# A hybrid encoder block: smaller first weight pieces, another load order and fewer zero products at the begin

## The chip, the cores and the metric

The kernel runs on one core of a Trainium2 chip. The metric is the device time of one execution in microseconds (us). Three runs of the kernel before took 1491.58, 1492.98 and 1494.12 us; the median is 1492.98 us.

## What is computed

The reference is one layer of an encoder trunk on 256 tokens of 2048 features, all in float32:

```python
u = _rms_norm(x, norm_mix_pre[l])
mix = hybrid_mixer(u, w_in[l], ...)          # proj = u @ w_in, three attention-like branches, @ w_out
x = x + _rms_norm(mix, norm_mix_post[l])
hdn = jnp.square(jax.nn.relu(_rms_norm(x, norm_mlp_pre[l]) @ w_mlp_up[l]))
x = x + _rms_norm(hdn @ w_mlp_down[l], norm_mlp_post[l])
```

Inside the mixer, `u @ w_in` gives the queries, keys and values of a stick-breaking attention and of a forgetting attention, the inputs of an RWKV-7 time mixing, and three gates. This case is about the first three column groups of that product only: 128 columns of `w_in` each, which are three heads of the stick-breaking queries.

## The kernel before

**Number format.** Every matrix product is made from float32 parts that TensorE reads in a shorter format. A weight tile `raw` (128 partitions x 1024 columns, 512 KB) is turned by ScalarE into a rounded copy `whi` (L158, at the begin L331) and by VectorE into the rest `wlo` = raw - whi (L159, at the begin L332). The activations are treated alike: `xsplit(k)` (L317) makes from feature tile k of x (128 features x 256 tokens) a tile `pk` of 512 columns, the rounded half by ScalarE (L242) and the rest by VectorE (L243). A full product is then `whi` with 512 columns of `pk` (a "hi" product, L340 at the begin) plus `wlo` with the first 256 columns (a "lo" product, L338).

**Staging.** All weights lie in one stack `wst` of 512 KB tiles in the order of use. A group of 128 output columns, a "unit", needs two tiles: one for the feature tiles 0 to 7, one for 8 to 15. In the steady part the helper `wnext` keeps one split weight tile ahead of TensorE, and SyncE's DMA queue (SP) loads three raw tiles ahead. VectorE, ScalarE and TensorE work side by side, and TensorE's order is the program's order.

**The begin.** x arrives in feature tiles and nothing is loaded yet. The first three units therefore share the feature tiles as they come: weight tiles 0, 2 and 4 hold the first halves of units 0, 1 and 2, tiles 1, 3 and 5 the second halves. The loop at L342 goes through the first eight feature tiles in two rounds of four. In a round, all three units take their 512-column piece of tiles 0, 2 and 4: `wpart(n, q)` splits the piece, `prods(n, ks, low)` issues one product for each feature tile. So a round has 12 hi and 12 lo products. Then each unit takes feature tiles 8 to 15 with its second weight tile (L358 to L371), unit 0 first: it needs feature tiles 8 to 15 split by VectorE one after the other.

**What sets the order.** The engines work through their queues in program order, and each piece of work waits for what it reads. SP issues the loads one after the other (L271 to L301): the parameters, the first pieces of weight tiles 0, 2, 4 (256 KB each), feature tiles 4 to 7 (512 KB), the second pieces, feature tiles 8 to 11, weight tile 1, and so on. ScalarE's own DMA queue issues feature tiles 0 and 1 and then 2 and 3 (L272). Eight counters are shared in turn by the DMAs of both queues, and a DMA waits at its issue for the one eight places before it.

**Zero products.** While nothing has arrived, TensorE multiplies a zeroed float32 tile by itself (L280): seven products of 256 columns, each of which the profile shows as two instructions. Their result is not used.

Of the kernel before, what the change touches and what calls it, by code (L numbers as in the profile page):

```python
# [17 lines left out]
T = 256  # L18
# [5 lines left out]
HALF = 1024  # L24
# [26 lines left out]
def hybrid_block(ctx, tc, xt, x, gains, params, consts, lora, gup, wst, out):  # L51
    nc = tc.nc
    V, A, G, PE = nc.vector, nc.scalar, nc.gpsimd, nc.tensor
# [11 lines left out]
    def nm(s):  # L65
        uid[0] += 1
        return f"{s}_{uid[0]}"
# [4 lines left out]
    def mps():  # L72
        return pm.tile([128, 512], F32, tag="mps", name=nm("mps"), bufs=4)
# [194 lines left out]
    def loadx(a, b, queue=nc.sync):  # L268
        return queue.dma_start(out=X0[:, a:b, :], in_=xt[:, a:b, :])

    nc.sync.dma_start(out=par, in_=params)  # L271
    for a in (0, 2):  # L272
        first_x = loadx(a, a + 2, nc.scalar)
    with tc.issue_after(first_x.ins):
        warm = A.activation(dum, dum, AF.Tanh)
    A6 = rp.tile([128, 6, T], F32, tag="b6", name="a6", bufs=1)
    zt = rp.tile([128, T], F32, tag="tha", name="zt", bufs=1)
    V.memset(zt, 0.0)
    idle = mps()
    for i in range(7):  # L280
        PE.matmul(idle[:, 0:T], zt[:, 0:128], zt, start=True, stop=True)
    raws = {}

    def load(n, q=None):

        if n not in raws:
            raws[n] = (rp.tile([128, HALF], F32, tag="m", name=nm("raw"), bufs=4) if n % 2 else
                       wpool.tile([128, HALF], F32, tag="raw", name=nm("raw"), bufs=3))
        cs = slice(0, HALF) if q is None else slice(512 * q, 512 * q + 512)
        nc.sync.dma_start(out=raws[n][:, cs], in_=wst[n][:, cs])  # L290

    for n in (0, 2, 4):
        load(n, 0)
    loadx(4, 8)
    for n in (0, 2, 4):
        load(n, 1)
    loadx(8, 12)
    load(1)
    loadx(12, 16)
    for n in (3, 5):  # L300
# [16 lines left out]
    def xsplit(k):  # L317
        u = pk()
        split(X0[:, k, :], u, P("g1", k))
        upk.append(u)  # L320
# [1 line left out]
    qb = [gps() for _ in range(3)]  # L322
    w = {}

    def wpart(n, q):
        if n not in w:
            w[n] = (wpool.tile([128, HALF], F32R, tag="whi", name=nm("whi"), bufs=3),
                    wpool.tile([128, HALF], F32R, tag="wlo", name=nm("wlo"), bufs=3))
        hi, lo = w[n]
        cs = slice(512 * q, 512 * q + 512)  # L330
        A.activation(hi[:, cs], raws[n][:, cs], AF.Copy)  # L331
        V.tensor_tensor(lo[:, cs], raws[n][:, cs], hi[:, cs].bitcast(F32), ALU.subtract)  # L332

    def prods(n, ks, low):
        for k in ks:
            i = k % 8
            if low:
                PE.matmul(qb[n // 2][:, 0:T], w[n][1][:, i * 128:i * 128 + 128], upk[k][:, 0:T], start=False, stop=k == 15)  # L338
            else:
                PE.matmul(qb[n // 2], w[n][0][:, i * 128:i * 128 + 128], upk[k], start=k == 0, stop=False)  # L340

    for q in range(2):  # L342
        ks = range(4 * q, 4 * q + 4)
        for k in ks[0:2]:
            xsplit(k)
        wpart(0, q)
        prods(0, ks[0:2], False)
        for k in ks[2:4]:
            xsplit(k)
        prods(0, ks[2:4], False)  # L350
        wpart(2, q)
        prods(2, ks, False)
        prods(0, ks, True)
        wpart(4, q)
        prods(4, ks, False)
        prods(2, ks, True)
        prods(4, ks, True)
    for k in range(8, 12):  # L358
        xsplit(k)
    for q in range(2):  # L360
        wpart(1, q)
    prods(1, range(8, 12), False)
    for k in range(12, 16):
        xsplit(k)
# [1 line left out]
    prods(1, range(8, 16), True)  # L366
    for n in (3, 5):
        for q in range(2):
            wpart(n, q)
        prods(n, range(8, 16), False)  # L370
        prods(n, range(8, 16), True)  # L371
    wpos[0] = 6
# [702 lines left out]
    c0 = g0 + 80  # L1075
# [558 lines left out]
    for g in range(4):  # L1634
# [8 lines left out]
        for tt, ps in enumerate(tok(hp, 3 if g == 3 else 1)):  # L1643
# [25 lines left out]
            with tc.issue_after(added.ins):  # L1669
                for c in (1024, 1536):  # L1670
                    cs = slice(c, c + 512)
# [131 lines left out]
```

## Time and the profile before

| what | value |
|---|---|
| median of three runs | 1492.98 us |
| the profiled execution | 1491.24 us, of which the span of its instructions is 1489.5 us |
| TensorE (PE) busy | 1476.4 us, 99% of the span |
| VectorE (DVE) busy | 1214.5 us, 82% |
| ScalarE (ACT) busy | 933.4 us, 63% |
| mean granted TensorE clock | 0.998 of full speed |

Times in the rows below are counted from the first instruction of the span. The profile names the engines PE (products), PEld (its weight loads), DVE, ACT, POOL and SP; a "q" behind an engine's name is its issuing part. The time between the span and the execution's own time, 1.74 us, lies before and after the kernel's instructions.

### The profile page before, as it was taken

What the parts mean: (1) busy time and instruction counts of PE and PEld (TensorE: products, weight loads), DVE (VectorE), ACT (ScalarE), POOL (GpSimd) and SP (SyncE); (2) the same over time, 40 slices, a digit from 0 to 9 for tenths busy, and PEclk for the clock granted to TensorE, in tenths of its full rate; (3) what the DMA queues carried; (4) which work ended last, traced back from release to release, by engine and by line L of the source; (5) the groups of instructions that cost most, each with busy time, mean ns of one, the idle gap of its engine ahead of it and who ended that gap; (6) DMA issues with size and microseconds to landing.
All of it is one profiled execution on the core that took longest, in us unless ns stands there. A gap on an engine that the chain in (4) does not pass through costs nothing.

```text
span 1489.5 us, 22848 instructions
## 1 busy us (share of the span) xinstructions
PE 1476.4 (99%) x8427; PEld 1248.4 (84%) x8427; DVE 1214.5 (82%) x1688; ACT 933.4 (63%) x1394; POOL 90.0 (6%) x160
## 2 busy tenths in 40 slices
PE   9999999999999999999999999999999999999997
PEld 8888888888778888788888888888888888888885
DVE  7676778999678898567647788999899999999986
ACT  7465666654576554474444777776767767777653
POOL 0011000100001100000000000000000000000000
PEclk9999999999999999999999999999999999999999
DMA  7545454545544546445855768888888887989874
GB/s 285 189 164 183 161 177 169 184 159 198 174 148 167 183 164 208 142 158 189 272 193 207 273 209 254 255 257 255 247 255 251 267 256 223 260 249 283 259 249 155
DMA packets 107759, 317.70 MB, mean 213 GB/s; under 512 B 10752, under 2 KB 14976, under 8 KB 107392
## 3 DMA queue, kind: packets, MB, share of 16 engines
q1 hardware_dynamic: 94688, 284.39, 55.4%
q0 software_dynamic: 8064, 29.36, 10.6%
q10 hardware_dynamic: 4896, 2.49, 0.6%
q8 instruction: 66, 1.08, 0.3%
q14 instruction: 45, 0.37, 0.1%
HBM read 282.65 MB, written 4.19 MB: 193 GB/s over the span
## 4 chain that ended last, share of the span: by engine, by line
PE 98%; DVE 1%; DMA 0%; issue 0%; ACT 0%; POOLq 0%; POOL 0%; DVEq 0%; ACTq 0%
PE gps L220 28%; PE gps L174 23%; PE gps L178 13%; PE gps L204 7%; PE mps L1511 3%; PE mps L1512 3%; PE mps L1513 3%; PE gps L1511 3%; PE gps L1513 3%; PE gps L1512 3%; PE gps L182 2%; PE gps L340 1%; PE mps L828 1%; PE gps L1270 0%; PE gps L338 0%; DMA x<-in_xt_dram 0%
## 5 line engine op out<-in xcount | busy, mean ns | idle before, releaser
L159 DVE TENSOR_TENSOR wlo<-raw,whi 128x1024 fp32r<-128x1024 f32 x495 | 600.9, 1221 | 154.2 <-ACT whi L158 139.4
L158 ACT ACTIVATE whi<-raw 128x1024 fp32r<-128x1024 f32 x495 | 521.5, 1057 | 253.9 <-PE gps L220 87.4
L174 PE MATMUL gps<-pk,whi 128*128 128x512 f32 x1321 | 332.4, 392 | 0.0
L220 PE MATMUL gps<-whi,pk 128*128 128x512 f32 x1136 | 286.4, 392 | 0.0
L174 PEld LDWEIGHTS gps<-pk,whi 128*128 128x128 f32 x1321 | 244.7, 188 | 47.6
L220 PEld LDWEIGHTS gps<-whi,pk 128*128 128x128 f32 x1136 | 211.4, 188 | 44.1 <-issue 0.4
L178 PEld LDWEIGHTS gps<-pk,wlo 128*128 128x128 f32 x1408 | 192.0, 190 | 13.6
L178 PE MATMUL gps<-pk,wlo 128*128 128x256 f32 x1408 | 196.9, 283 | 0.0
L220 PE MATMUL gps<-wlo,pk 128*128 128x512 f32 x568 | 155.3, 392 | 0.0
L220 PEld LDWEIGHTS gps<-wlo,pk 128*128 128x128 f32 x568 | 105.7, 188 | 22.0
L1374 DVE TENSOR_TENSOR sp<-raw,sp 128x1024 fp32r<-128x1024 f32 x67 | 81.7, 1220 | 3.4 <-ACT sp L1373 3.1
L1402 ACT ACTIVATE sp<-gps 128x512 f32<-128x512 f32 x52 | 31.1, 598 | 84.3 <-PE gps L182 84.3
L1373 ACT ACTIVATE sp<-raw 128x1024 fp32r<-128x1024 f32 x67 | 70.7, 1055 | 14.1 <-PE mps L1512 5.1
L204 PE MATMUL gps<-whi,pk 128*128 128x512 f32 x256 | 68.9, 390 | 0.0
L1511 PE MATMUL mps<-whi,fm 128*128 128x512 f32 x168 | 66.2, 394 | 0.0
L1512 PE MATMUL mps<-whi,fm 128*128 128x512 f32 x168 | 65.8, 392 | 0.0
L1513 PE MATMUL mps<-wlo,fm 128*128 128x512 f32 x168 | 65.6, 390 | 0.0
L1473 POOL DMA_DIRECT2D raw<-raw x40 | 35.0, 874 | 427.4 <-DVE raw L1470 108.4
L204 PEld LDWEIGHTS gps<-whi,pk 128*128 128x128 f32 x256 | 47.8, 188 | 9.9
L1511 PE MATMUL gps<-whi,fm 128*128 128x512 f32 x126 | 49.3, 391 | 0.0
L1513 PE MATMUL gps<-wlo,fm 128*128 128x512 f32 x126 | 49.1, 390 | 0.0
L1470 DVE TENSOR_TENSOR raw<-raw,raw 128x1024 f32<-128x1024 f32 x40 | 48.8, 1220 | 0.4
(400 smaller groups left out, 2013.4 us busy)
## 6 DMA issues: line engine op xcount, KB each, us to landing
raw<-in_wst_dram SPq DMA_DIRECT2D x499, 512.0 KB, 4.4
raw<-raw POOLq DMA_DIRECT2D x40, 512.0 KB, 6.4
sp<-in_wst_dram SPq DMA_DIRECT2D x16, 512.0 KB, 5.3
raw<-sp POOLq DMA_DIRECT2D x8, 512.0 KB, 6.2
sp<-raw POOLq DMA_DIRECT2D x8, 512.0 KB, 6.4
x<-in_x_dram SPq DMA_DIRECT2D x8, 256.0 KB, 5.5
xs<-x SPq DMA_DIRECT2D x2, 1024.0 KB, 4.8
x<-xs SPq DMA_DIRECT2D x4, 512.0 KB, 6.5
```

The source lines that it names most:

```text
L158: A.activation(hi, raw, AF.Copy)
L159: V.tensor_tensor(lo, raw, hi.bitcast(F32), ALU.subtract)
L174: PE.matmul(ps, hi[:, i * 128:i * 128 + 128], pks[i], start=first and i == 0, stop=False)
L178: PE.matmul(ps[:, 0:T], lo[:, i * 128:i * 128 + 128], pks[i][:, 0:T], start=False, stop=False)
L204: PE.matmul(ps[tt], pks[k][:, c:c + 128], w[:, (k - k0) * 512:(k - k0) * 512 + 512], start=k == 0 and part == 0 and w is hl[0], stop=w is ...
L220: PE.matmul(ps[tt], pks[k][:, c:c + 128], w[:, (k - k0) * 512:(k - k0) * 512 + 512], start=k == 0 and part == 0 and w is hl[0], stop=False)
L1373: A.activation(hi, raw, AF.Copy)
L1374: V.tensor_tensor(lo, raw, hi.bitcast(F32), ALU.subtract)
L1470: V.tensor_tensor(x, x, z, ALU.add)
L1511: PE.matmul(Q[f], p, w, start=d == 0 and i == 0, stop=False)
L1512: PE.matmul(Q[f], pl, w, start=False, stop=False)
L1513: PE.matmul(Q[f], p, wl, start=False, stop=d == nd - 1 and i == 1)
```

## The change

Feature tiles 2 and 3 are loaded by SP instead of ScalarE's queue. The first 512 columns of weight tiles 0, 2 and 4 are loaded and split in two pieces of 256 columns (128 KB) each, and the order of SP's loads is: first pieces, feature tiles 2 and 3, second pieces, feature tiles 4 to 7, third pieces (512 columns). The loop over rounds now has three rounds, of two, two and four feature tiles. The zero products are four of 256 columns and one of 128. The sum of products and of bytes is the same.

```diff
-    for a in (0, 2):
-        first_x = loadx(a, a + 2, nc.scalar)
+    first_x = loadx(0, 2, nc.scalar)
@@
-    for i in range(7):
-        PE.matmul(idle[:, 0:T], zt[:, 0:128], zt, start=True, stop=True)
+    for i in range(5):
+        PE.matmul(idle[:, 0:T // (1 + i // 4)], zt[:, 0:128], zt[:, 0:T // (1 + i // 4)], start=True, stop=True)
@@
-    def load(n, q=None):
+    def load(n, c0=0, c1=HALF):
...
-        cs = slice(0, HALF) if q is None else slice(512 * q, 512 * q + 512)
+        cs = slice(c0, c1)
         nc.sync.dma_start(out=raws[n][:, cs], in_=wst[n][:, cs])
 
     for n in (0, 2, 4):
-        load(n, 0)
+        load(n, 0, 256)
+    loadx(2, 4)
+    for n in (0, 2, 4):
+        load(n, 256, 512)
     loadx(4, 8)
     for n in (0, 2, 4):
-        load(n, 1)
+        load(n, 512)
     loadx(8, 12)
@@
-    def wpart(n, q):
+    def wpart(n, c0, c1):
...
-        cs = slice(512 * q, 512 * q + 512)
+        cs = slice(c0, c1)
@@
-    for q in range(2):
-        ks = range(4 * q, 4 * q + 4)
+    for k0, k1 in ((0, 2), (2, 4), (4, 8)):
+        ks = range(k0, k1)
         for k in ks[0:2]:
             xsplit(k)
-        wpart(0, q)
+        wpart(0, 128 * k0, 128 * k1)
         prods(0, ks[0:2], False)
-        for k in ks[2:4]:
+        for k in ks[2:]:
             xsplit(k)
-        prods(0, ks[2:4], False)
-        wpart(2, q)
+        prods(0, ks[2:], False)
+        wpart(2, 128 * k0, 128 * k1)
         prods(2, ks, False)
         prods(0, ks, True)
-        wpart(4, q)
+        wpart(4, 128 * k0, 128 * k1)
         prods(4, ks, False)
         prods(2, ks, True)
         prods(4, ks, True)
```

SP's queue before, from its first load to the last piece of the second round (raw_101, raw_103 and raw_105 are weight tiles 0, 2 and 4; x_85 holds all feature tiles, 512 columns being two of them):

```order
L271 DMA par<-in_params_dram 128x116
L290 DMA raw_101<-in_wst_dram 128x512
L290 DMA raw_103<-in_wst_dram 128x512
L290 DMA raw_105<-in_wst_dram 128x512
L269 DMA x_85<-in_xt_dram 128x1024
L290 DMA raw_101<-in_wst_dram 128x512
L290 DMA raw_103<-in_wst_dram 128x512
L290 DMA raw_105<-in_wst_dram 128x512
```

The same stretch of SP's queue after the change (raw_98, raw_100 and raw_102 are weight tiles 0, 2 and 4):

```order
L271 DMA par<-in_params_dram 128x116
L289 DMA raw_98<-in_wst_dram 128x256
L289 DMA raw_100<-in_wst_dram 128x256
L289 DMA raw_102<-in_wst_dram 128x256
L269 DMA x_85<-in_xt_dram 128x512
L289 DMA raw_98<-in_wst_dram 128x256
L289 DMA raw_100<-in_wst_dram 128x256
L289 DMA raw_102<-in_wst_dram 128x256
L269 DMA x_85<-in_xt_dram 128x1024
L289 DMA raw_98<-in_wst_dram 128x512
L289 DMA raw_100<-in_wst_dram 128x512
L289 DMA raw_102<-in_wst_dram 128x512
```

Feature tiles 4 to 7 (128x1024) have moved from the fifth place to the ninth.

ScalarE before, from feature tile 2 to the first piece of the second round (pk tiles are the split feature tiles):

```order
L242 ACTIVATE pk_144<-x_85,par 128x256
L242 ACTIVATE pk_147<-x_85,par 128x256
L331 ACTIVATE whi_152<-raw_103 128x512
L331 ACTIVATE whi_164<-raw_105 128x512
L242 ACTIVATE pk_180<-x_85,par 128x256
L242 ACTIVATE pk_183<-x_85,par 128x256
L331 ACTIVATE whi_138<-raw_101 128x512
```

ScalarE after the change, from feature tile 2 to the first piece of the third round:

```order
L242 ACTIVATE pk_163<-x_85,par 128x256
L242 ACTIVATE pk_166<-x_85,par 128x256
L333 ACTIVATE whi_139<-raw_98 128x256
L333 ACTIVATE whi_145<-raw_100 128x256
L333 ACTIVATE whi_153<-raw_102 128x256
L242 ACTIVATE pk_187<-x_85,par 128x256
L242 ACTIVATE pk_190<-x_85,par 128x256
L333 ACTIVATE whi_139<-raw_98 128x512
```

Three pieces of 256 columns stand where two of 512 stood, and from feature tile 4 (pk_180 before, pk_187 now) the order is the old one, on VectorE too. Behind the begin no engine's order differs.

## Rows read from the trace of the kernel before

**Rows 1.** The page, busy time of each engine and its instructions.

```profile
PE 1476.4 (99%) x8427; PEld 1248.4 (84%) x8427; DVE 1214.5 (82%) x1688; ACT 933.4 (63%) x1394; POOL 90.0 (6%) x160
```

**Rows 2.** Waits of PE, whole span: waiter, releaser, us in total, times, longest.

```profile
PE gps L340 <- DVE pk L243: 0.9, 1, 0.9
PE mps L1255 <- DVE x L1217: 0.5, 1, 0.5
```

**Rows 3.** The chain that ended last, 0 to 80 us: start us, us, what.

```profile
1.18 5.59 DMA x<-in_xt_dram
...
7.88 1.82 PE gps L340 x6
...
12.06 1.84 PE gps L340 x8
```

**Rows 4.** Timeline of ACT, 0.7 to 18.9 us: start us, us, what, idle time before.

```profile
3.58 0.91 ACT L242 ACTIVATE pk<-x,par 128x256 fp32r<-128x256 f32 x2 [0.42 <-DMA x<-in_xt_dram]
5.37 0.63 ACT L331 ACTIVATE whi<-raw 128x512 fp32r<-128x512 f32 x1 [0.88 <-DMA raw<-in_wst_dram]
6.80 0.91 ACT L242 ACTIVATE pk<-x,par 128x256 fp32r<-128x256 f32 x2 [0.80 <-DMA x<-in_xt_dram]
...
8.99 0.91 ACT L242 ACTIVATE pk<-x,par 128x256 fp32r<-128x256 f32 x2 [0.24 <-DMA x<-in_xt_dram]
9.81 0.61 ACT L331 ACTIVATE whi<-raw 128x512 fp32r<-128x512 f32 x1
...
12.19 1.71 ACT L242 ACTIVATE pk<-x,par 128x256 fp32r<-128x256 f32 x4
```

**Rows 5.** Timeline of DVE, 0.8 to 19 us.

```profile
4.12 0.89 DVE L243 SCALAR_TENSOR_TENSOR pk<-x,par,pk 128x256 fp32r<-128x256 f32 x2 [0.46 <-ACT pk L242]
...
8.26 1.29 DVE L332 TENSOR_TENSOR wlo<-raw,whi 128x512 fp32r<-128x512 f32 x2
9.54 0.88 DVE L243 SCALAR_TENSOR_TENSOR pk<-x,par,pk 128x256 fp32r<-128x256 f32 x2
...
11.06 0.88 DVE L243 SCALAR_TENSOR_TENSOR pk<-x,par,pk 128x256 fp32r<-128x256 f32 x2
...
15.85 1.67 DVE L243 SCALAR_TENSOR_TENSOR pk<-x,par,pk 128x256 fp32r<-128x256 f32 x4
```

**Rows 6.** Timeline of PE, 0 to 19 us.

```profile
1.18 5.38 PE L281 MATMUL mps<-zt 128*128 128x256 f32 x14 [1.18 <-DVE zt L278]
...
11.90 2.00 PE L340 MATMUL gps<-pk,whi 128*128 128x512 f32 x8
...
16.09 2.01 PE L340 MATMUL gps<-pk,whi 128*128 128x512 f32 x8
```

**Rows 7.** Windows: us, busy of PE, PEld, DVE, ACT, POOL, PEclk, DMA share, GB/s.

```profile
0.00:3.50 3.50, 2.32 (x6) 1.87 (x7) 0.54 (x4) 1.49 (x2) 2.18 (x15) 1.00 0.45 135
3.50:6.50 3.00, 3.00 (x11) 2.51 (x10) 1.52 (x4) 1.54 (x3) 0.00 (x0) 1.00 0.98 298
6.50:9.00 2.50, 1.65 (x7) 0.91 (x6) 1.84 (x5) 1.95 (x5) 0.00 (x0) 1.00 1.02 370
...
12.00:17.00 5.00, 5.00 (x29) 4.34 (x28) 5.00 (x11) 5.00 (x13) 0.00 (x0) 1.00 1.02 419
```

**Rows 8.** Timeline of SP, 0 to 9.4 us: the issues of its DMAs.

```profile
1.17 1.37 SPq L290 DMA_DIRECT2D raw<-in_wst_dram  x3
2.58 0.44 SPq L269 DMA_DIRECT2D x<-in_xt_dram  x1
3.06 1.72 SPq L290 DMA_DIRECT2D raw<-in_wst_dram  x3
```

**Rows 9.** The tile of x, 0 to 15 us: time of its DMAs from issue to landing.

```profile
DMA to landing us min/median/max: 2.8/6.4/7.5
```

**Rows 10.** The line of the zero products: duration in ns min/median/max, first and last start.

```profile
L281 PE MATMUL mps<-zt x14: 378/634/792, 1.2 to 6.2; 128*128 128x256 f32 x14
```

**Rows 11.** Timeline of PE, 3.0 to 5.1 us.

```profile
2.62 2.77 PE L281 MATMUL mps<-zt 128*128 128x256 f32 x6
```

More of the change, by code (lines that the diff above doesn't have):

```diff
@@ L360, in hybrid_block @@
     for q in range(2):
-        wpart(1, q)
+        wpart(1, 512 * q, 512 * q + 512)
     prods(1, range(8, 12), False)
@@ L368, in hybrid_block @@
         for q in range(2):
-            wpart(n, q)
+            wpart(n, 512 * q, 512 * q + 512)
         prods(n, range(8, 16), False)
```

## The prediction

> **What bounds the kernel now.** I read the busy times first. TensorE is busy for 1476.4 of 1489.5 us [rows 1], so only 13 us of the span could be won without removing products. The waits of TensorE come next: apart from its start they are 0.9 us at the first products, at 7.88 us, and 0.5 us at L1255, far behind this change [rows 2]. The chain of work that ended last agrees. It runs through the load of x, from 1.18 to 6.78 us, through the split of feature tiles 2 and 3, and from 7.88 us through TensorE [rows 3]. So whatever the change brings must come from the time before 7.88 us, and it must survive the stretch in which TensorE still waits for freshly made operands.
>
> What feeds TensorE there is read in the timelines. ScalarE waits for feature tile 0 until 3.58, for the first weight piece until 5.37, for feature tile 2 until 6.80 and for feature tile 4 until 8.99 us [rows 4]. Each of these waits ends with a landing. From 8.99 us on it goes on without a gap, and VectorE from 9.54 us: in the window from 12 to 17 us both are busy for 5.00 of 5.00 us [rows 4, 5, 7]. So there are two limits in turn, the loads up to feature tile 4, and ScalarE and VectorE behind it. TensorE does not show the second one, because it starts late enough.
>
> **Unchanged work.** A hi product takes 1.84 / 8 = 0.23 us [rows 3]. A round of four feature tiles takes 16.09 - 11.90 = 4.19 us [rows 6]. The three new rounds hold the same products, the first two together 4.19 us and the third another 4.19 us. No byte is added.
>
> **Zero products.** At first their records start (2.77 - 0.634) / 5 = 0.427 us apart [rows 10, 11]. The change leaves nine of the fourteen records, the ninth at the same pace as the others or shorter. They end at about 1.18 + 9 x 0.427 + 0.2 (pipeline, 0.634 - 0.427) = 5.2 us, where they now last until 6.56 us [rows 6]. Cutting them saves nothing by itself. Kept at seven, they would hold the first product until 6.2 us, and that would be hidden behind round 3, as shown below.
>
> **Rounds 1 and 2: cost nothing, gain nothing that lasts.** By the windows 3.5 x 135 = 472 kB have moved by 3.5 us, 298 GB/s follow until 6.5 us and 370 GB/s until 9 us [rows 7]. Feature tiles 4 to 7 are the last of 1850 KB = 1894 kB: parameters 58 KB, feature tiles 0 to 3 512 KB, pieces 768 KB, and their own 512 KB. By those rates 1894 kB have moved at 6.5 + (1894 - 1366) / 370 = 7.93 us, and ScalarE starts on them at 8.99 [rows 4]: landing comes 1.06 us after the mean byte. With the same rates and lag the changed order lands the first pieces at 4.5, 4.9 and 5.4 us, feature tiles 2 and 3 at 6.25 and the second pieces at 6.7, 7.1 and 7.6 us. Splitting two feature tiles takes ScalarE 0.91 us [rows 4]. A 256-column piece is not in these rows. It lies between half of the 0.61 us of 512 columns and all of it; I take 0.4, near the half. VectorE has the second feature tile split at 4.12 + 0.89 = 5.01 us [rows 5]. So the first product comes at about 5.2 us, round 1 ends at 7.3, round 2 starts at 7.55 and ends at about 9.65 us. At the upper price ScalarE would be through at 8.8 and VectorE at 9.4 us, both before feature tile 4 needs them at 8.99 and 9.54. So more instructions, at either price, cost nothing.
>
> **Round 3: where the gain is taken back.** It needs feature tiles 4 to 7, as the old second round did, and the order on ScalarE and VectorE from there is the old one. If they land when they did, the first weight piece is ready at 9.81 + 0.61 = 10.42 us [rows 4]. TensorE waits from 9.65 to 10.46. Feature tiles 6 and 7 are split on VectorE at 11.54 and 11.94 us (11.06 + 0.48, then 0.40 more) [rows 5]. So the fourth product starts at 11.98, and the rest of the round, 4.19 - 3 x 0.23 = 3.50 us, ends at 15.48 instead of 16.09. That is 0.61 us ahead. Then unit 0 takes feature tiles 8 to 15. VectorE ends the last of them at 15.85 + 1.67 = 17.52 us [rows 5], so its product starts at 17.56; before, it started at 16.09 + 7 x 0.23 = 17.70 [rows 6]. Only 0.14 us is left. The 2.5 us by which TensorE could start earlier are used up by a VectorE that was full already. **The gain is 0.14 us plus whatever feature tiles 4 to 7, and what follows them, land earlier.**
>
> **How much earlier do they land?** The bytes ahead of them are the same, so only the rate counts. The alternation of two queues ends earlier, since feature tiles 2 and 3 leave ScalarE's queue. At 419 GB/s from 3.5 us on, the best rate [rows 7], they land at 3.5 + 1422 / 419 + 1.06 = 7.95 us, 1.04 earlier. At 370 it is 8.40, 0.59 earlier. On the other side SP issues a piece every (2.58 - 1.17) / 3 = 0.47 us [rows 8], and 131 kB in 0.47 us are 279 GB/s; at that rate for all that stands ahead of them, then 370, they land at 9.20, 0.21 later. I take 0.3 us earlier, half way between the unchanged time and the 370 that a single queue showed. So the gain is 0.14 + 0.3 = 0.45 us, with ends of -0.07 and 1.18. Behind the begin no order differs, and TensorE's later waits follow its own work, so the shift is kept to the end.
>
> The Trainium skill speaks against the smaller pieces: its page "DMA: Bandwidth & Descriptors", section "Bandwidth", wants DMAs batched to 1 MiB and gives each about 2.0 us plus bytes at 436 GB/s. As an estimate from that page, six pieces one after the other would take 13.8 us against 7.8 us for three of twice the size, and the kernel would be 6.0 us slower. The trace does not bear that out as a sum: 1850 KB land by 8.99 us, which DMAs queued one behind the other could not do, so the fixed parts overlap.
>
> **The sum.** The profiled execution was 1491.24 us, of which 1489.5 are the span; it becomes 1490.8 and 1489.05. The median of the three runs stands 1.74 us above the profiled execution, so the forecast there is 1492.98 - 0.45 = **1492.5 us**. A difference under 0.2%, 3.0 us, is about what a measurement of this kernel cannot tell from no change.
>
> **Rivals.**
> *The start is gained whole.* TensorE runs unbroken from 5.2 us and comes to round 3 at 9.4 instead of 11.90: 2.5 us, 1490.5 us. For it: TensorE is the bound everywhere else [rows 1]. Against it: feature tiles 4 to 7 would have to land about 2.4 us earlier, and the best rate gives 1.04. Chance 0.05; even this is under 0.2%.
> *Feature tiles 4 to 7 come late (slower).* Their issue moves from 2.58 us behind three smaller pieces, feature tiles 2 and 3 and a second set: the second set's place ends at 3.06 + 1.72 = 4.78 [rows 8], 2.2 us later. If their landing is bound to their issue, by the median of 6.4 us [rows 9] they land at 11.2: 2.2 - 0.14 = 2.1 us slower, 1495.0 us; by the largest, 7.5, at 12.3, which is 3.2 us slower, 1496.1 us. It decides as soon as they land after 8.99 + 0.14 = 9.13 us. Against it: the DMA engines are 0.98 to 1.02 busy from 3.5 us on [rows 7], so those times are mostly queueing. The page's rule on batching is this rival in other words. Chance 0.15, and 0.03 for its part over 3.0 us.
> *The clock rises later.* The zero products' records shrink from 634 to 378 ns [rows 10]; the granted clock is written as 1.00 even in the first window [rows 7], so I go by the durations, which mean 1.2 and then 2.4 GHz. Thirteen steps take 5.0 us, ten to eleven of them at 0.427, so the rise came at about 5.5 us, 4.3 us after the first zero product. With fewer of them the gap before the first real product might make TensorE earn it anew, from 5.2 to 9.5 us. At half speed 4.3 us do 2.15 of the 4.19 us, and rounds 1 and 2 end at 11.5 instead of waiting until 10.46. Round 3 is then unbroken, still 0.4 us ahead: 1492.6 us. Another 4.3 us at half speed would cost 2.15 more, 1494.7 us. The Trainium skill, "TensorE: Matmul & The Clock Gate", Part 1, says that the throttled state is the default and sustained activity releases it. The trace agrees, from 634 to 378 ns. Chance 0.06.
>
> **How the numbers follow.** The forecast's own case, gains of -0.07 to 1.18 us, has 0.72; with half the spread of the runs (2.54 / 2 = 1.3 us) it reaches from 1490.5 to 1494.3. The whole gain lies at its lower edge. Taking in the first third of the late case, up to 1.5 us slower, gives 1490.5 to 1494.5. Faster by over 0.2% is none of the cases; 0.02 stays for what I did not see. Slower by over 0.2% is 0.03 of the late case and 0.01 of the clock: 0.04. No difference: 0.94.
>
> **What would show it.** Right: first products at 5.1 to 5.5 us; feature tile 4 split from 8.0 to 9.2; a wait of TensorE of 0.4 to 1.0 us at the start of round 3, and smaller ones at feature tiles 6, 7 and 12 to 15; VectorE without a gap from feature tile 4 on; unit 0's last hi product 0.1 to 1.2 us earlier than 17.70. Wrong: round 3 without a wait, feature tile 4 after 9.2 us, real products at half pace past 6 us, or a difference that arises behind 20 us.

## The result, and the profile after

| | before | changed |
|---|---|---|
| median of 21 runs each | 1492.75 us | 1494.86 us |
| lowest and highest | 1491.58 to 1494.12 | 1493.12 to 1496.55 |
| the profiled execution, its span | 1491.24, 1489.5 us | 1494.96, 1493.2 us |

The ratio is 1.0013, with a 95% interval of 1.0007 to 1.0018. The changed kernel is slower by about 1.9 us (1.0 to 2.7). That is less than the 0.2% named as the bound of what can be told, but 21 runs do tell it, and the median lies 0.36 us above the predicted range.

The spans differ by 3.7 us, more than the medians, because the profiled execution of before was 1.5 us below its median of 21 runs and that of the changed kernel was at its own. 1.71 us of the 3.7 arise in the begin and stand unchanged from 18 to 51 us. The rest comes in steps at places that the change doesn't touch: the shift is 1.94 us at 60 us, 2.46 at 700 and 3.4 to 3.7 behind 1400.

The page of the changed kernel, busy times as in [rows 1]:

```profile
PE 1477.5 (99%) x8423; PEld 1246.7 (83%) x8423; DVE 1215.2 (81%) x1691; ACT 934.0 (63%) x1397; POOL 90.2 (6%) x160
```

The waits of PE over the whole span, as in [rows 2]. Two waits of 1.2 us in all, for ScalarE's weight pieces, are new, and those for VectorE's feature tiles grew from 0.9 to 1.2 us:

```profile
PE gps L342 <- DVE pk L243: 1.2, 2, 0.8
PE gps L342 <- ACT whi L333: 1.2, 2, 0.8
```

The chain that ended last, as in [rows 3], from 0 to 21 us:

```profile
4.02 0.43 SPq L289
...
4.49 6.22 DMA x<-in_xt_dram
...
13.34 1.82 PE gps L342 x6
```

Before, it began with the load of feature tiles 2 and 3 and was on TensorE from 7.88 us. Now it runs through SP's issues until 4.49 us, through the load of feature tiles 4 to 7, and reaches TensorE at 13.34 us. SP's issues, as in [rows 8], show why that load starts so late:

```profile
1.17 1.37 SPq L289 DMA_DIRECT2D raw<-in_wst_dram  x3
2.58 0.43 SPq L269 DMA_DIRECT2D x<-in_xt_dram  x1
3.06 1.39 SPq L289 DMA_DIRECT2D raw<-in_wst_dram  x3
4.49 0.43 SPq L269 DMA_DIRECT2D x<-in_xt_dram  x1
4.97 1.93 SPq L289 DMA_DIRECT2D raw<-in_wst_dram  x3
```

An issue takes the same 0.47 us for 128 KB (1.17 to 2.58, three of them) as for 256 KB before, and one of 512 KB takes no longer (4.49 to 4.97). Feature tiles 4 to 7 are issued at 4.49 instead of 2.58 us, and they land 6.2 us after issue, as they did before (6.4).

ScalarE, as in [rows 4]:

```profile
5.18 0.42 ACT L333 ACTIVATE whi<-raw 128x256 fp32r<-128x256 f32 x1 [0.26 <-DMA raw<-in_wst_dram]
...
7.76 0.91 ACT L242 ACTIVATE pk<-x,par 128x256 fp32r<-128x256 f32 x2 [0.77 <-DMA x<-in_xt_dram]
8.57 1.20 ACT L333 ACTIVATE whi<-raw 128x256 fp32r<-128x256 f32 x3
10.74 0.91 ACT L242 ACTIVATE pk<-x,par 128x256 fp32r<-128x256 f32 x2 [0.96 <-DMA x<-in_xt_dram]
...
13.92 1.71 ACT L242 ACTIVATE pk<-x,par 128x256 fp32r<-128x256 f32 x4
```

Feature tile 4 is split at 10.74 instead of 8.99 us, 1.75 later, and feature tiles 8 to 11 at 13.92 instead of 12.19, 1.73 later. VectorE, as in [rows 5], ends feature tiles 12 to 15 later by 1.74 us:

```profile
9.10 1.13 DVE L334 TENSOR_TENSOR wlo<-raw,whi 128x256 fp32r<-128x256 f32 x3
...
17.59 1.67 DVE L243 SCALAR_TENSOR_TENSOR pk<-x,par,pk 128x256 fp32r<-128x256 f32 x4
```

TensorE, as in [rows 6]. It starts real products at 5.04 us and so earlier than before (6.21), and waits four times in what follows:

```profile
5.04 1.33 PE L342 MATMUL gps<-pk,whi 128*128 128x512 f32 x4
...
7.04 0.73 PE L342 MATMUL gps<-pk,whi 128*128 128x512 f32 x2 [0.43 <-ACT whi L333]
...
9.03 1.20 PE L342 MATMUL gps<-pk,whi 128*128 128x512 f32 x4 [0.79 <-ACT whi L333]
...
12.22 0.73 PE L342 MATMUL gps<-pk,whi 128*128 128x512 f32 x2 [0.83 <-DVE pk L243]
13.34 1.82 PE L342 MATMUL gps<-pk,whi 128*128 128x512 f32 x6 [0.39 <-DVE pk L243]
...
19.65 1.11 PE L340 MATMUL gps<-pk,wlo 128*128 128x256 f32 x8
```

The last row is the meter used below: the first lo product of unit 0 over feature tiles 8 to 15. It starts at 19.65 us; before, at 17.94. The windows, as in [rows 7], show how many bytes moved when:

```profile
0.00:3.50 3.50, 2.31 (x6) 1.87 (x7) 0.55 (x4) 1.49 (x2) 2.18 (x15) 1.00 0.43 136
3.50:6.50 3.00, 3.00 (x12) 2.27 (x10) 1.80 (x5) 1.63 (x4) 0.00 (x0) 1.00 0.79 233
6.50:9.00 2.50, 1.31 (x7) 0.90 (x6) 1.12 (x3) 1.66 (x5) 0.00 (x0) 1.00 1.00 258
9.00:12.00 3.00, 2.36 (x12) 1.90 (x12) 1.95 (x6) 1.96 (x5) 0.00 (x0) 1.00 0.99 367
```

The last of these windows in the kernel before:

```profile
9.00:12.00 3.00, 3.00 (x21) 2.69 (x20) 2.96 (x7) 3.00 (x7) 0.00 (x0) 1.00 1.05 417
```

From 3.5 to 6.5 us the DMA engines are busy for 0.79 of the time where they were for 0.98, and move 233 GB/s instead of 298: 195 kB less. From 6.5 to 9 us they count as fully busy and still move only 258 instead of 370, 280 kB less, and from 9 to 12 us 367 instead of 417, 150 kB less. Together that is about 625 kB, or 1.5 us at 417 GB/s; less than a third of it falls into the window in which the engines were partly idle.

### The profile page after: what moved, and what is told of

The parts are those of the page before. It is cut to its first block, busy times and chain, and to the rows that moved or that the text cites. A ratio compares the mean times of both kernels' runs of the same rounds, so it can differ in the third digit from the quotient of the medians.

```text
span 1493.2 us, 22854 instructions
## 1 busy us (share of the span) xinstructions
PE 1477.5 (99%) x8423; PEld 1246.7 (83%) x8423; DVE 1215.2 (81%) x1691; ACT 934.0 (63%) x1397; POOL 90.2 (6%) x160
## 3 DMA queue, kind: packets, MB, share of 16 engines
HBM read 282.65 MB, written 4.19 MB: 192 GB/s over the span
## 4 chain that ended last, share of the span: by engine, by line
PE 95%; DVE 2%; issue 1%; DMA 1%; ACT 1%; SPq 0%; POOLq 0%; POOL 0%; DVEq 0%; ACTq 0%
PE gps L220 28%; PE gps L174 23%; PE gps L178 13%; PE gps L204 7%; PE mps L1513 3%; PE mps L1514 3%; PE mps L1515 3%; PE gps L1515 2%; PE gps L1513 2%; PE gps L1514 2%; PE gps L182 2%; DVE wlo L159 1%; PE mps L830 1%; PE gps L342 1%; DMA raw<-raw 1%
```

## The experiments

**Theory: issue.** SP hands over one DMA per 0.47 us, of 128 KB as of 512 KB. The smaller pieces stand first, so fewer bytes are in the DMA engines' hands early: by 3.5 us parameters 58, feature tiles 0 to 3 512, four pieces of 128, in all 1082 KB, where before it was 58 + 512 + 3 x 256 + 512 + 256 = 2106 KB. **Rivals:** each DMA has a fixed price; rows of 1 KB or the stride in memory move slowly; the new rounds cost time on ScalarE and VectorE; fewer zero products leave TensorE at its lower clock for longer.

All traces, with the bytes issued by 3.5 us (from the timelines of SP and ScalarE's queue) and the landings by the trace's DMA records:

| kernel | KB by 3.5 us | feature tiles 4-7: issue, landing | 8-11 landing | lo product of unit 0 | median us | ratio to before, 95% interval |
|---|---|---|---|---|---|---|
| before | 2106 | 2.58, 8.97 | 12.17 | 17.94 | 1492.75 | 1 |
| changed | 1082 | 4.49, 10.72 | 13.90 | 19.65 | 1494.86 | 1.0013 [1.0007, 1.0018] |
| E1 | 1210 | 4.38, 9.33 | 13.45 | 19.00 | 1494.31 | 1.0010 [1.0001, 1.0019] |
| E2 | 2106 | 2.59, 9.18 | 12.36 | 18.56 | 1494.14 | 1.0008 [0.9999, 1.0017] |
| E3 | 2106 | 2.58, 8.71 | 11.91 | 17.66 | 1493.94 | 1.0010 [1.0001, 1.0019] |
| E3b | 2106 | 2.58, 8.80 | 11.99 | 18.48 | 1494.32 | 1.0009 [1.0000, 1.0018] |
| E4 | 1082 | 4.57, 10.64 | 13.84 | 21.18 | 1497.00 | 1.0026 [1.0016, 1.0036] |
| E5 | 1082 | 4.96, 9.62 | 13.49 | 19.04 | 1494.62 | 1.0010 [1.0001, 1.0019] |
| E6 | 2106 | 2.67, 8.86 | 12.04 | 17.80 | 1492.93 | 0.9996 [0.9987, 1.0005] |
| E7 | 1082 | 4.62, 10.74 | 14.04 | 19.67 | 1495.26 | 1.0012 [1.0004, 1.0021] |
| E8 | 1210 | 5.22, 10.69 | 13.87 | 19.62 | 1494.66 | 1.0014 [1.0005, 1.0023] |
| E9 | 1082 | 5.08, 10.82 | 14.21 | 19.77 | 1494.37 | 1.0011 [1.0002, 1.0019] |
| E11 | 2106 | 2.11, 8.84 | 12.26 | 21.33 | 1495.77 | 1.0023 [1.0013, 1.0033] |
| E12 | 1354 | 4.85, 10.36 | 13.61 | 19.30 | 1495.63 | 1.0019 [1.0010, 1.0028] |
| F1 | 1594 | 2.59, 7.93 | 12.64 | 18.20 | 1493.68 | 1.0005 [0.9996, 1.0014] |
| F2 | 1850 | 4.38, 10.65 | 11.90 | 18.43 | 1492.87 | 1.0005 [0.9996, 1.0014] |
| F3 | 1082 | 4.70, 10.70 | 13.88 | 20.57 | 1495.30 | 1.0015 [1.0006, 1.0025] |
| F4 | 1082 | 4.60, 10.60 | 13.79 | 19.53 | 1494.67 | 1.0012 [1.0003, 1.0021] |

Each ratio is against runs of the kernel before on the same chip, whose median was 1492.75 to 1493.35 us from set to set. It need not be the quotient of two medians: E3's 1493.94 us over the 1493.35 of its set would be 1.0004, where the ratio is 1.0010.

Each landing is that of one profiled execution. Kernels with the loads of before (before, E2, E3, E3b) have feature tiles 8 to 11 at 11.91 to 12.36 us, those with the loads of the change (changed, E4, E9, F3, F4) at 13.79 to 14.21. So a difference under 0.45 us between two rows says little.

### Parts of the change

**E1, feature tiles 2 and 3 back on ScalarE's queue**, all else as changed.

```diff
-    first_x = loadx(0, 2, nc.scalar)
+    for a in (0, 2):
+        first_x = loadx(a, a + 2, nc.scalar)
...
-    loadx(2, 4)
```

> The change with feature tiles 2 and 3 put back on ScalarE's DMA queue, beside the six 128 KB pieces on SP. Meters: the start of feature tile 4's split on ScalarE (8.99 us before, 10.74 after the change) and the first lo product of unit 0 over feature tiles 8 to 15 on TensorE (17.94 before, 19.65 after). If SP as the only issuer is the cause (a DMA every 0.47 us, DMA share 0.49 at 4.5 to 5 us), one issue fewer on SP and a second issuer bring most back: split at 9.0 to 9.6, lo product at 18.0 to 18.5, time 1493.0. If the 256-column pieces themselves are what moves badly, they still do: split at 10.3 to 10.8, lo product at 19.2 to 19.7, time 1494.5.

Feature tiles 4 to 7 landed 1.4 us earlier than in the changed kernel, but the next ones, 8 to 11, only 0.45 us earlier, and so did unit 0 (0.65). Taking one DMA off SP does not undo the delay. The run fits neither side cleanly. Its windows show that it did not lose where the theory looks first:

```profile
3.50:6.50 3.00, 2.23 (x7) 1.67 (x6) 1.68 (x6) 1.61 (x4) 0.00 (x0) 1.00 1.11 322
...
9.00:12.00 3.00, 3.00 (x18) 2.64 (x17) 2.36 (x6) 2.65 (x6) 0.00 (x0) 1.00 1.01 333
```

From 3.5 to 6.5 us it moves more than the kernel before (322 against 298 GB/s); it falls behind later, with 333 against 417 GB/s from 9 to 12 us and the DMA engines counted as busy all the time.

**E2, the new rounds and zero products with the old loads**, feature tiles 2 and 3 on ScalarE's queue too.

```diff
...
-        load(n, 0, 256)
-    loadx(2, 4)
-    for n in (0, 2, 4):
-        load(n, 256, 512)
+        load(n, 0, 512)
```

> Three rounds with 256-column splits and 4.5 zero products, but the loads of before (512-column pieces, feature tiles 2 and 3 on ScalarE's queue, 4 to 7 in fifth place). If the loads alone are the cause: feature tile 4 split at 9.0, lo product at 17.8 to 18.0, time within 0.3 us of before, 1492.8. If the rounds cost something themselves (twelve split instructions instead of six, or the clock): split at 9.0 but lo product at 18.5 or later, time 1493.5 or more.

Feature tiles 8 to 11 are back at 12.36, within 0.2 us of before: the loads are what came late, not the rounds. But unit 0 is 0.62 us later, at 18.56 us, which is the second expectation's side, and so is the time. In the order of the new rounds ScalarE splits the first pieces of all three weight tiles ahead of feature tile 2, and these pieces of 256 KB were there at 6.63, 7.29 and 7.94 us (before: 5.35, 6.98 and 7.68). So it came to feature tile 4, landed at 9.18 us, only at 9.66:

```profile
9.66 0.89 ACT L242 ACTIVATE pk<-x,par 128x256 fp32r<-128x256 f32 x2
```

So the rounds are not free when feature tile 4 lands early. How much of the 0.62 us is theirs, and how much comes from the first piece that was later in this execution, is not shown.

**E3 and E3b, the zero products alone**: the kernel before with `range(5)` and the half-width fifth product, in two sets.

> The kernel before with 4.5 zero products instead of 7 and nothing else. By the load theory: nothing, first product at 6.1, feature tile 4 split at 9.0, lo product at 17.94, time 1492.8. By the clock theory (the clock rises later with fewer zero products): products at half pace past 6 us, and up to 2 us slower, 1494.7.

> The kernel before with 4.5 zero products, once more, for its runs. If fewer zero products let the clock rise later in some runs, again some runs show a mean clock of 0.996 or less, which no run of the kernel before did, and the median is 0.3 to 0.8 us above before. If the first set was chance: clocks of 0.997 and 0.998 only, and a median within 0.2 us of before.

No load is later than before, and yet both sets came out 1.0010 and 1.0009. TensorE's timeline in the second:

```profile
5.96 4.05 PE L340 MATMUL gps<-pk,whi 128*128 128x512 f32 x8 [0.56 <-ACT whi L331]
```

Eight hi products last 4.05 us where at full pace they take 2.00 [rows 6]: they ran at 1.2 GHz until 10.47 us. In the first set's profile the clock had risen at 5.85 us, and unit 0 was on time. So with fewer zero products the moment of the rise varies, and can cost 0.8 us at unit 0 (18.48 against 17.66). The mean clock was 0.996 in two of the eleven runs of E3 and in one of E3b, and never below 0.997 in those of the kernel before beside them. By the clock records of all traces the first rise came between 4.03 and 6.94 us in all ten with seven zero products. In the eight with 4.5 it came by 6.56 us in five, and at 9.75 (E1), 10.47 (E3b) and 13.30 us (E4) in three.

**E4, the old two rounds with the new loads**, zero products as changed.

```diff
-    for k0, k1 in ((0, 2), (2, 4), (4, 8)):
+    for k0, k1 in ((0, 4), (4, 8)):
```

> Two rounds of four feature tiles with 512-column splits as before, but the loads of the change (six 128 KB pieces, all on SP but feature tiles 0 and 1). If the loads alone are the cause: feature tile 4 split at 10.7, lo product at 19.5 to 19.8, time 1494.5 to 1495.0. If the rounds carry a part of it, less: split at 10.7 but lo product before 19.2.

```profile
8.81 3.78 PE L342 MATMUL gps<-pk,whi 128*128 128x512 f32 x8 [3.42 <-ACT whi L333]
```

The first product came only at 8.81 us, behind a wait of 3.42 us, and the clock rose at 13.3. This is the slowest of all, 1.0026, and unit 0 is 1.5 us later than in the changed kernel, outside both expectations. That is not the price of the long rounds alone: eight hi products took 3.78 us where they take 2.00 at full pace. At full pace the 4.19 us of the first round would have ended at 13.0 us, when the changed kernel still waited (13.34). So the late clock alone is large enough for the 1.5 us; whether the short rounds help by keeping TensorE at work, and so the clock up, is not shown.

### Why the loads came late

**E5, three more DMAs in the kernel before**, each first piece in two halves of 64 partitions, rows of 2 KB as before.

```diff
-        nc.sync.dma_start(out=raws[n][:, cs], in_=wst[n][:, cs])
+        for r in ((slice(0, 64), slice(64, 128)) if q == 0 else (slice(0, 128),)):
+            nc.sync.dma_start(out=raws[n][r, cs], in_=wst[n][r, cs])
```

> The kernel before, but each of the first three 256 KB pieces is loaded by two DMAs of 64 partitions each: six DMAs of 128 KB as in the change, with rows of 2 KB as before. Meters: landing of feature tiles 8 to 11 (issue to landing puts it at 12.17 us before, 13.90 after the change, 13.45 and 13.84 in the two experiments with 256-column pieces) and unit 0's first lo product (17.94 before, 19.65 after). If the number of DMAs that SP issues is the cause (0.47 us each): feature tiles 8 to 11 land at 13.2 or later, lo product 18.8 or later. If the rows of 1 KB are the cause: 12.0 to 12.5 and 17.8 to 18.2, time as before.

```profile
1.18 3.74 SPq L291 DMA_DIRECT2D raw<-in_wst_dram  x6
4.96 0.58 SPq L269 DMA_DIRECT2D x<-in_xt_dram  x1
```

**E6, rows of 1 KB in the kernel before, with its three DMAs.** The host lays the two halves of each first piece one behind the other, so one DMA reads 256 rows of 1 KB. The second pieces lie behind them, contiguous as well.

```diff
...
+        if q == 0:
+            src = wst[n].rearrange("p c -> (p c)")[0:65536].rearrange("(b p c) -> p b c", b=2, c=256)
+            nc.sync.dma_start(out=raws[n][:, cs].rearrange("p (b c) -> p b c", b=2), in_=src)
+            return
...
```

> The kernel before, with three DMAs for the three first pieces as before, but each made of 256 rows of 1 KB (the host lays the two column halves of those pieces one behind the other). If the number of DMAs is the cause: feature tiles 8 to 11 land at 12.0 to 12.5, lo product at 17.8 to 18.2, time as before. If rows of 1 KB are the cause: landing at 13.0 or later, lo product 18.6 or later, time 1494.3 or more.

```profile
3.50:6.50 3.00, 3.00 (x10) 2.38 (x8) 1.32 (x5) 1.57 (x4) 0.00 (x0) 1.00 1.05 364
```

**E7, the changed kernel with every small piece contiguous in memory**, laid so by the host.

```diff
-        nc.sync.dma_start(out=raws[n][:, cs], in_=wst[n][:, cs])
+        src = wst[n][:, cs]
+        if c1 - c0 < HALF:
+            src = wst[n].rearrange("p c -> (p c)")[128 * c0:128 * c1].rearrange("(p c) -> p c", c=c1 - c0)
+        nc.sync.dma_start(out=raws[n][:, cs], in_=src)
...
```

> The change, with every piece of weight tiles 0, 2 and 4 in one unbroken run of the memory instead of 1 KB out of every 4 KB. If the stride of the source is what makes the 256-column pieces move badly: feature tile 4 split at 9.0 to 9.6 (10.74 after the change), lo product 18.0 to 18.6, time 1493.3. If it is the size or the number of the DMAs: split at 10.3 to 10.9, lo product 19.2 to 19.8, time 1494.8.

These three belong together. Three more DMAs with the long rows give most of the delay (13.49 instead of 12.17). They also took SP 0.63 us each, from 1.18 to 4.96 for six, so they held it longer than the 0.47 us of whole pieces. Short rows with three DMAs give no delay, and the window from 3.5 to 6.5 us even moves 364 GB/s. Contiguous pieces change nothing of it (14.04). It is the DMAs that SP has to issue ahead, not the row and not the stride.

**E12, three DMAs that carry almost nothing.** The kernel before with an 8 KB load behind each first piece.

```diff
         load(n, 0)
+        nc.sync.dma_start(out=cpool.tile([128, 16], F32, name=nm("extra")), in_=params[:, 0:16])
```

> The kernel before with three more DMAs of 8 KB on SP, one behind each of the first three weight pieces, into tiles that nothing reads. No piece is split and next to no byte is added. By the issue theory three DMAs more cost 1.3 us: feature tiles 8 to 11 at 13.3 to 13.6 us, unit 0's lo product at 18.8 to 19.2, time 1.0 to 1.5 us more. If splitting the pieces is what costs (smaller transfers, more completions that somebody waits for): 12.1 to 12.5, lo product 17.9 to 18.2, time as before.

```profile
1.65 0.42 SPq L294 DMA_DIRECT2D extra<-in_params_dram  x1
2.12 0.43 SPq L290 DMA_DIRECT2D raw<-in_wst_dram  x1
...
3.07 0.43 SPq L290 DMA_DIRECT2D raw<-in_wst_dram  x1
4.47 0.33 SPq L294 DMA_DIRECT2D extra<-in_params_dram  x1
```

8 KB hold SP for the same 0.47 us (1.65 to 2.12). The third extra load should have been issued at 3.54 and went out at 4.47 us. It is the ninth DMA and waits for feature tiles 0 and 1, eight places before it, at their shared counter. With 24 KB more to move, feature tiles 8 to 11 landed 1.44 us later. So SP's time, its issues and that wait, is enough for most of the delay. The landing, 13.61, and the lo product, 19.30, are close to the first expectation; the time, 1.0019 or 2.8 us, is about twice what it said, and why is not shown.

**E8, two issuers.** The changed kernel with seven zero products; ScalarE's queue issues feature tiles 0 and 1, weight tile 2's first piece and feature tiles 2 and 3.

```diff
...
-        load(n, 0, 256)
...
+            load(n, c, c + 256, nc.scalar if n == 2 and c == 0 else nc.sync)
+            if n == 2 and c == 0:
+                last_x = loadx(2, 4, nc.scalar)
...
```

> The change with seven zero products, feature tiles 2 and 3 and the first 128 KB piece of weight tile 2 issued by ScalarE's queue, the other five pieces by SP. As many DMAs as the change, but two fewer of them on SP ahead of feature tiles 4 to 7. If what costs is SP's issuing (about 0.43 us for each DMA that SP issues ahead, as three DMAs more gave 1.3 us and four 1.73): feature tiles 8 to 11 land at 12.8 to 13.2 us (13.90 after the change, 12.17 before), lo product of unit 0 at 18.4 to 18.9, time 1494.0. If every DMA costs that wherever it is issued: landing at 13.7 to 14.0, lo product 19.4 or later.

The landing, 13.87, and the lo product, 19.62, are those of the second case. The waits of SP's queue from 0 to 6 us:

```profile
SPq L287 <- DMA x<-in_xt_dram: 1.8, 1, 1.8
```

The ninth DMA came up early, and waited 1.8 us at the shared counter for feature tiles 0 and 1. SP stood still, only 1210 KB were out by 3.5 us, and nothing was won. So the run can't tell the two cases apart: the queue that should have been relieved was held by the counter.

**E11, one DMA fewer on SP in the kernel before**: ScalarE's queue issues the parameters, between its two loads of x.

> The kernel before with the load of the parameters issued by ScalarE's queue between feature tiles 0, 1 and 2, 3, so that SP begins with the first weight piece: one DMA fewer on SP. By the issue theory everything behind it comes 0.43 us earlier: feature tiles 8 to 11 at 11.7 us, unit 0's lo product at 17.4 to 17.6 instead of 17.94, time 0.4 us less than before. By its rival (the DMA engines, not the issuing, set the pace in the kernel before): 12.0 to 12.2, lo product 17.8 to 18.0, time as before.

```profile
5.99 0.91 ACT L242 ACTIVATE pk<-x,par 128x256 fp32r<-128x256 f32 x2 [2.34 <-DMA par<-in_params_dram]
```

Feature tiles 4 to 7 were issued 0.47 us earlier and landed 0.13 us earlier, 8 to 11 no earlier (12.26). In the kernel before, issue does not bind: the DMA engines have enough to do. The time itself tells nothing here, since the parameters landed at 5.90 us and every split waited for them. Behind a wait of TensorE of 1.5 us the clock fell to 0.50 here too, from 10.14 to 13.56 us, with all seven zero products.

**F1, small pieces, but feature tiles 4 to 7 issued between the two sets.** Seven zero products, feature tiles 2 and 3 on ScalarE's queue, the new rounds.

```diff
...
     for n in (0, 2, 4):
         load(n, 0, 256)
-    loadx(2, 4)
+    loadx(4, 8)
     for n in (0, 2, 4):
         load(n, 256, 512)
-    loadx(4, 8)
```

> Six 128 KB pieces, but feature tiles 4 to 7 (512 KB) stay in fifth place on SP, issued at 2.6 us between the two sets, and feature tiles 2 and 3 on ScalarE's queue; seven zero products. If what costs is that little data has been handed to the DMA engines early (1338 KB by 4.5 us after the change, about 1850 KB by 3.6 us before): feature tiles 8 to 11 land at 12.0 to 12.5 us as before, in spite of the six pieces. If every further DMA on SP costs its own time wherever it stands: 13.3 to 13.7 us. The products themselves may come later here, since the second set lands behind feature tiles 4 to 7; the landing is the meter.

```profile
3.50:6.50 3.00, 3.00 (x9) 2.37 (x8) 1.74 (x6) 1.73 (x4) 0.00 (x0) 1.00 0.99 286
6.50:9.00 2.50, 2.50 (x14) 2.12 (x13) 2.21 (x6) 2.27 (x7) 0.00 (x0) 1.00 1.05 394
```

All six small pieces are there, and the DMA engines are full again, 0.99 and 1.05, since 512 KB more are in their hands by 3 us. Feature tiles 8 to 11 land 0.47 us later than before instead of 1.73, nearer to the first expectation than to the second. A fixed price for each small DMA, or one for each DMA on SP wherever it stands, would not have gone away. (By its timelines the kernel before has handed over 1850 KB by 3.0 us and 2362 by 3.6, more than the expectation says.)

**F2, feature tiles 4 to 7 late, but no more DMAs.** The kernel before, with `loadx(4, 8)` behind the second set of 256 KB pieces.

> The kernel before with feature tiles 4 to 7 behind the second set of 256 KB pieces: not one DMA more, and as many bytes handed over early, but feature tiles 4 to 7 are issued at about 4.1 us instead of 2.6. If the bytes handed over early decide: feature tiles 4 to 7 land last of that group, at 10.6 to 11.0 us (their bytes now come behind 768 KB more), and feature tiles 8 to 11 at 12.0 to 12.5 as before. If it is the number of DMAs alone: the same 12.0 to 12.5. If the late issue of feature tiles 4 to 7 by itself holds up what follows: 13.3 or later.

```profile
10.68 3.31 ACT L242 ACTIVATE pk<-x,par 128x256 fp32r<-128x256 f32 x8 [0.60 <-DMA x<-in_xt_dram]
```

They land at 10.65 us, as late as in the changed kernel, but feature tiles 8 to 11 are there at 11.90, and ScalarE takes all eight in one row. Unit 0 is 0.49 us late instead of 1.71. So their own late landing is not most of the loss; the whole stream behind it must be late.

### The zero products in the changed kernel

**E9 and F4, the changed kernel with seven zero products, and F3, the changed kernel again** beside F4.

```diff
-    for i in range(5):
-        PE.matmul(idle[:, 0:T // (1 + i // 4)], zt[:, 0:128], zt[:, 0:T // (1 + i // 4)], start=True, stop=True)
+    for i in range(7):
+        PE.matmul(idle[:, 0:T], zt[:, 0:128], zt, start=True, stop=True)
```

> The change with the seven zero products of before. By the load theory alone the time stays at that of the change, 1494.9, and the lo product at 19.6: the first real product is 1.1 us later, at 6.2 us, and rounds 1 and 2 still end before round 3 can start. If fewer zero products cost something in runs in which the clock rises late, as the spread of the run with zero products alone suggests (0.6 us slower in the median, 1498.27 us in the worst run), it is 0.5 us faster than the change, 1494.3, and no run has a clock under 0.997.

> The change once more, beside the next kernel on the same chip. 1.6 to 2.4 us slower than the kernel before; feature tiles 8 to 11 land at 13.7 to 14.0 us and unit 0's first lo product starts at 19.5 to 19.9 us.

> The change with seven zero products once more. By the load theory the same as the kernel beside it within 0.4 us, since rounds 1 and 2 wait for feature tiles 4 to 7 in either case. If the zero products carry a part of the loss, as they do by about 0.6 to 1.5 us when they alone are cut in the kernel before, it is faster than the kernel beside it by that much.

The windows of F3, whose clock fell again:

```profile
12.00:13.40 1.40, 0.81 (x3) 0.38 (x3) 1.37 (x4) 1.40 (x5) 0.00 (x0) 0.99 1.02 402
13.40:16.80 3.40, 3.40 (x10) 2.80 (x11) 3.05 (x7) 3.40 (x9) 0.00 (x0) 0.50 1.02 419
```

The same stretch of F4:

```profile
13.40:16.80 3.40, 3.40 (x19) 2.79 (x20) 3.40 (x8) 3.40 (x8) 0.00 (x0) 1.00 1.02 418
```

In F3 TensorE had waited 1.8 us, was granted 0.50 (1.2 GHz) from 13.4 to 16.8 us and did 10 products where F4 did 19. Unit 0 came at 20.57 against 19.53 us. The mean clock of the eleven runs of F4 was 0.998 each time, that of F3 between 0.996 and 0.998. But the medians differ by only 0.63 us, and the intervals, 1.0015 [1.0006, 1.0025] and 1.0012 [1.0003, 1.0021], overlap. E9, with seven as well, was 1.0011. So the late loads with all seven zero products stand at 1.0011 and 1.0012, with fewer at 1.0013 and 1.0015: the loads are enough for most of the loss, and what fewer zero products add to them, some 0.6 us by the medians, is not settled. In the kernel before, fewer zero products alone gave 1.0010 and 1.0009: the two losses do not add up. That a TensorE which waits for loads anyway has less to lose by a low clock would fit, but is not shown.

## Why the prediction was wrong

**The step that failed** is "How much earlier do they land?". It said "The bytes ahead of them are the same, so only the rate counts" and took 0.3 us earlier, with an end of 0.21 later at the rate of SP's issues. Measured: 1.75 us later. The rates were 233 and 258 GB/s, below the 279 of that end, where I had carried over 298 and 370 of before. They had been the rates of engines that had 2106 KB at 3.5 us. The changed order hands over 1082 KB by then. In the table the landing of feature tiles 8 to 11 falls into groups by that number: 11.9 to 12.4 us with 1850 KB or more, 12.64 with 1594, 13.45 to 14.2 with 1354 or fewer. Inside the last group it does not follow it, and the moment was chosen afterwards: by 5 us the changed kernel has handed over 2106 KB and F1 1850, yet F1's landing is 1.26 us earlier. The argument against the rival, that DMA engines busy for 0.98 to 1.02 make it "mostly queueing", was true of the old order alone.

That the DMAs issued ahead make the stream late is shown by runs: E5 and E12 add such DMAs to the kernel before and get most of the delay, E6 and E7 rule out rows and stride, F1 keeps the small pieces and loses most of the delay. How they do it is shown in part only: the idle share of the engines from 3.5 to 6.5 us covers less than a third of the bytes that were missing, and E1, which moved more than the kernel before in that window, was late all the same.

The Trainium skill, "DMA: Bandwidth & Descriptors", section "Bandwidth", wants DMAs batched to 1 MiB, and its direction was right. The price of 2.0 us plus bytes at 436 GB/s stands in another section of that page of the Trainium skill, "Anatomy of one DMA — SWDGE (gpsimd) path", as a fit for a DMA issued from GpSimd. The estimate of 6.0 us, made from it for pieces one after the other, does not hold for DMAs queued on SP: 1.7 us were measured, and 0.47 in F1.

**What held.** "The gain is 0.14 us plus whatever feature tiles 4 to 7, and what follows them, land earlier" was right in kind. With 1.73 later it gives 1.59 us slower; unit 0 was 1.71 us later, so of the 0.14 us hardly anything showed, and the medians differ by 2.11 us. The early start indeed did not last: TensorE began at 5.04 us (5.2 predicted) and gave it back in waits. A 256-column split took 0.42 us (0.4), and VectorE is still the second limit: its last split stood 1.74 us later and unit 0 with it.

That rounds 1 and 2 "cost nothing" came true by luck. It rested on the same rates: feature tiles 2 and 3 landed at 7.74 us instead of 6.25, and the second pieces at 8.07 to 9.33 instead of 6.7 to 7.6. ScalarE was through with them at 9.77 us and VectorE at 10.23, later than the 8.8 and 9.4 of the upper price and too late for a feature tile 4 at its old 8.99. Only because that tile was itself late did it not show; in E2, where it was not, unit 0 was 0.62 us late. The forecast wait at the start of round 3, 0.4 to 1.0 us, was 0.83, but it ended at 12.22 us and not at 10.46.

**The rival that came true** is "Feature tiles 4 to 7 come late (slower)", to which I gave 0.15. Its 2.1 us and 1495.0 us, from the median of 6.4 us between issue and landing, compare with 2.11 and 1494.86; the measured 10.72 us are past its point of decision, 9.13. It named the DMA for which the chain then showed it. That the sums agree so closely is luck: it had the landing at 11.2 us, unit 0 was 1.71 us later, and the other 0.4 us of the medians arise elsewhere. What it lacked is that the whole stream is late: F2 has feature tiles 4 to 7 as late and loses little.

**The clock.** "Cutting them saves nothing by itself" was right, that it costs nothing was not shown: E3 and E3b have no later load and stand at 1.0010 and 1.0009, with intervals that reach down to 1.0001 and 1.0000. In one of their profiles the clock rose at 10.47 us. The rival "The clock rises later" was priced for the changed kernel, where it stays unsettled. The Trainium skill, "TensorE: Matmul & The Clock Gate", Part 1, calls the throttled state the default that activity releases, and F3's fall to 0.50 agrees.

**Open.** Why only 258 GB/s from 6.5 to 9 us, with engines busy for 1.00, is not explained. In the packet records of the trace those of 4 KB took 229 ns on average there, though half of them took 159 or less; before it was 175 on average. So the busy share counts stretches in which packets took longer. The steps behind 51 us, 2.0 us in the profiled executions, are not explained either; a difference behind 20 us was one of the signs of a wrong forecast. Why E3's time moved although its profile shows unit 0 on time isn't shown: its other runs may be like E3b's, but they have no profile. No version was measurably faster than the kernel before; E6 (0.9996) and F2 (1.0005) can't be told from it.

## What to carry to other kernels

At the begin, write beside each DMA its issue time and add up the bytes handed over by then: here small pieces first meant 1082 KB instead of 2106 by 3.5 us, and everything behind them landed some 1.7 us later. The DMA engines were partly idle for a while, but most of the loss came after, so a busy share near 1 is no proof that nothing is lost; the GB/s beside it tells more. Rates read from the old trace need not hold when fewer bytes are queued. Before making an engine start earlier, look at the next engine that is already full; where that one sets the pace, an earlier first product is given back, while a later landing is passed on whole.

## What the runs showed of the hardware

- SP issued one DMA per 0.47 us for 8, 128, 256 and 512 KB alike where nothing held it (E12, changed, before), but one of 64 partitions per 0.63 us (E5).
- The DMA engines' busy share can be 1.00 at 258 GB/s (changed, 6.5 to 9 us) and 1.05 at 417 (before, 9 to 12 us).
- With first pieces of 1 KB rows the window from 3.5 to 6.5 us moved 364 GB/s, with 2 KB rows 298 (E6, before).
- A DMA can wait at its issue for the counter of the one eight places before: 1.8 us in E8, 0.9 us in E12, with all behind it on SP.
- The 58 KB of parameters, issued second on ScalarE's queue behind 256 KB, landed only at 5.90 us (E11), and held up the first split by 2.3 us.
- TensorE's clock fell to 0.50 again at 13.4 us, behind a wait of 1.8 us, though it had risen at 6.56 us (F3); the same at 10.14 us behind one of 1.5 us, with seven zero products (E11).
